# Rotary embedding in fp32: part of one store on GpSimd's queue, and three rows in one GpSimd product

## The chip, the cores and the metric

The kernel runs on one core of a Trainium2 chip. Such a core has four engines that compute (TensorE, VectorE, ScalarE, GpSimd), a SyncE that issues transfers here, and sixteen DMA engines that move the data. In the profile these are PE (and PEld for its weight loads), DVE, ACT, POOL and SP. The metric is the device time of one execution in microseconds (us), lower is better. The time before is the median of three runs.

## The reference

The input `x` is 16 batches of 512 positions of 1024 numbers in fp32, that is, 16 heads of 64. In each head the first 32 numbers and the last 32 are rotated against each other by tables that depend on the position alone:

```python
x = x.reshape(batch, seq, num_heads, head_dim)          # 16, 512, 16, 64
x1, x2 = (x[..., :half_dim], x[..., half_dim:])
cos = cos[None, :, None, :]                             # from (512, 32)
sin = sin[None, :, None, :]
rotated = np.concatenate([x1 * cos - x2 * sin, x1 * sin + x2 * cos], axis=-1)
```

32 MiB come in, 32 MiB go out, with two products and one sum for each number.

## The kernel before

The kernel cuts the work into 8 tiles of 4 MiB. A tile has 128 partitions (2 batches by 64 groups of positions), and a partition has 8 rows (positions) of 1024 numbers, 32 KB in all. Five tiles are held at a time. Loads and stores are issued by SyncE, in the order of the program:

```python
NB, BUFS, BANK = 2, 5, 512
PAIRS = ((1, 2), (4, 5), (6, 7))
EXTRA = 5

xp = ...tile_pool(name="xp", bufs=BUFS)                 # tiles of x, 32 KB a partition
bp = ...tile_pool(name="bp", bufs=3)                    # products with sin, 8 KB a partition

load(0, 0, FIRST[0])                                    # rows 0 to 2 of tile 0
... sin and cos tables, the other rows of tile 0 ...
for t in range(1, BUFS):
    load(t)                                             # tiles 1 to 4
spare = fixed.tile([1, EXTRA, 16], FP32)
for i in range(EXTRA):                                  # transfers of 64 bytes
    nc.sync.dma_start(out=spare[:1, i], in_=sin_v[:1, :16])
```

The identity matrix that TensorE needs is made by GpSimd. TensorE spreads the tables over 128 partitions and VectorE writes the signed sine table (L116, L117); GpSimd's products wait for that.

The work on one tile is split by rows. For the pairs of rows (1, 2), (4, 5) and (6, 7) GpSimd multiplies the swapped halves by the sine (`sin_rows`, L165), VectorE multiplies by the cosine into PSUM (`pair_product`, L141) and adds the two (`pair_sum`, L189). Row 3 gets its sine product from GpSimd too; VectorE's cosine product goes into a half-row PSUM buffer, TensorE adds GpSimd's product to it by a matmul with the identity, and ScalarE copies the sum back (`pe_half`, one half of the row at a time, one buffer). Row 0 does without GpSimd. The order in a tile:

```python
for t in range(NT):
    first, second, third = PAIRS
    b1 = sin_rows(t, first[0], 2)
    p1 = pair_product(t, first[0])
    ... row 0: VectorE's product, TensorE's sums, ScalarE's copy ...
    b3 = sin_rows(t, ROW_PE, 1)                         # row 3
    b2 = sin_rows(t, second[0], 2)                      # rows 4 and 5
    pair_sum(*p1, b1)
    h0, h1 = zip(parts(rows(t, ROW_PE)), parts(b3))
    pe_half(ROW_PE, *h0)
    p2 = pair_product(t, second[0])
    b1 = sin_rows(t, third[0], 2)                       # rows 6 and 7
    pair_sum(*p2, b2)
    pe_half(ROW_PE, *h1)
    p1 = pair_product(t, third[0])
    if t + 1 < NT:
        cos_product(own_ps, rows(t + 1, ROW_OWN), ROW_OWN)
    pair_sum(*p1, b1)
    stores(t)

def stores(t):                                          # cut: one store of the whole tile
    store(t, 0, KK)
    if t + 1 == NT - BUFS:                              # after store 2
        for n in range(BUFS, NT):
            load(n)                                     # tiles 5, 6 and 7
```

So the transfers follow each other as: loads 0 to 4, stores 0 to 2, loads 5 to 7, stores 3 to 7.

Of the kernel before, what the change touches and what calls it, by code (L numbers as in the profile page):

```python
# [8 lines left out]
FP32 = mybir.dt.float32  # L9
BF16 = mybir.dt.bfloat16  # L10
# [4 lines left out]
BANK = 512  # L15


ROW_OWN, ROW_PE = 0, 3

PAIRS = ((1, 2), (4, 5), (6, 7))  # L20

FIRST = (3, 8)
LAST_OUT = (8,)

EXTRA = 5


@with_exitstack
def kernel(
# [13 lines left out]
    nc = tc.nc  # L43
    P = nc.NUM_PARTITIONS
    batch, seq, dim = x.shape
# [3 lines left out]
    PB = P // NB  # L49
    KK = seq // PB  # L50
    NT = batch // NB
    F = KK * dim

    x_v = x.rearrange("(t b) (p k) d -> t (b p) (k d)", b=NB, k=KK)
    out_v = out.rearrange("(t b) (p k) h d -> t (b p) (k h d)", b=NB, k=KK)
    cos_v = cos.rearrange("(p k) j -> p (k j)", k=KK)
    sin_v = sin.rearrange("(p k) j -> p (k j)", k=KK)

    fixed = ctx.enter_context(tc.tile_pool(name="fixed", bufs=1))
    xp = ctx.enter_context(tc.tile_pool(name="xp", bufs=BUFS))  # L60
    bp = ctx.enter_context(tc.tile_pool(name="bp", bufs=3))
    pfix = ctx.enter_context(tc.tile_pool(name="pfix", bufs=1, space=bass.MemoryType.PSUM))
    pe = ctx.enter_context(tc.tile_pool(name="pe", bufs=1, space=bass.MemoryType.PSUM))
    pd = ctx.enter_context(tc.tile_pool(name="pd", bufs=1, space=bass.MemoryType.PSUM))
# [3 lines left out]
    tiles = [None] * NT  # L68

    def load(t, lo=0, hi=KK):  # L70
        if tiles[t] is None:
            tiles[t] = xp.tile([P, F], FP32, name="xt")
        s = slice(lo * dim, hi * dim)
        nc.sync.dma_start(out=tiles[t][:, s], in_=x_v[t][:, s])  # L74

    def store(t, lo=0, hi=KK):
        s = slice(lo * dim, hi * dim)
        nc.sync.dma_start(out=out_v[t][:, s], in_=tiles[t][:, s])

    load(0, 0, FIRST[0])  # L80
    tabs = bp.tile([P, 2 * dim], FP32, name="b")
# [3 lines left out]
    nc.sync.dma_start(out=cos_sb, in_=cos_v)  # L85
    for lo, hi in zip(FIRST, FIRST[1:]):
        load(0, lo, hi)
    for t in range(1, BUFS):
        load(t)
    spare = fixed.tile([1, EXTRA, 16], FP32)  # L90
    for i in range(EXTRA):
        nc.sync.dma_start(out=spare[:1, i], in_=sin_v[:1, :16])

    ident = fixed.tile([P, P], FP32)
    make_identity(nc, ident)
    zero = fixed.tile([P, BANK], BF16)
    nc.vector.memset(zero, 0.0)  # L97
    own_ps = pe.tile([P, dim], FP32)
    pe_ps = pe.tile([P, BANK], FP32)
    for ps in (own_ps[:, :BANK], own_ps[:, BANK:], pe_ps):  # L100
# [3 lines left out]
    tab = pfix.tile([P, BANK], FP32)  # L104
    cos_t = tab[:, : KK * half]
    sin_t = tab[:, KK * half : 2 * KK * half]
    spread = fixed.tile([PB, P], FP32)
    eye = ident[:PB, :PB]
    nc.vector.tensor_copy(
        out=spread.rearrange("p (b q) -> p b q", b=NB),  # L110
        in_=bass.AP(tensor=eye.tensor, offset=eye.offset, ap=[eye.ap[0], [0, NB], [1, PB]]),
# [12 lines left out]
    def swapped(r):  # L124
        n = r.shape[1] // hd
        return bass.AP(tensor=r.tensor, offset=r.offset + half, ap=[r.ap[0], [hd, n], [-half, 2], [1, half]])

    def rows(t, k, n=1):
        return tiles[t][:, k * dim : (k + n) * dim]

    def cos_product(out, r, k, n=1):

        c = cos_t[:, k * half : (k + n) * half]
        m = r.shape[1] // (n * half)
        if n == 1:
            cb = bass.AP(tensor=c.tensor, offset=c.offset, ap=[c.ap[0], [0, m], [1, half]])
            o, i = (z.rearrange("p (a j) -> p a j", j=half) for z in (out, r))
        else:
            cb = bass.AP(tensor=c.tensor, offset=c.offset, ap=[c.ap[0], [half, n], [0, m], [1, half]])
            o, i = (z.rearrange("p (k a j) -> p k a j", k=n, j=half) for z in (out, r))  # L140
        nc.vector.tensor_tensor(out=o, in0=i, in1=cb, op=ALU.mult)  # L141

    def own_product(r):

        s = bass.AP(
            tensor=own_t.tensor,
            offset=own_t.offset + half,
            ap=[own_t.ap[0], [0, nh], [-half, 2], [1, half]],
        )
        nc.vector.tensor_tensor(out=heads(r), in0=heads(r), in1=s, op=ALU.mult)  # L150

    def sin_product(out, r, k, n):
        s = sns[:, k : k + n].rearrange("p k a j -> p (k a j)")
        if n == 1:
            sb = bass.AP(tensor=s.tensor, offset=s.offset, ap=[s.ap[0], [0, nh], [1, hd]])
            o, i = heads(out), swapped(r)
        else:
            sb = bass.AP(tensor=s.tensor, offset=s.offset, ap=[s.ap[0], [hd, n], [0, nh], [1, hd]])
            o = out.rearrange("p (k h a j) -> p k h a j", k=n, a=2, j=half)
            i = bass.AP(  # L160
                tensor=r.tensor,
                offset=r.offset + half,
                ap=[r.ap[0], [dim, n], [hd, nh], [-half, 2], [1, half]],
            )
        nc.gpsimd.tensor_tensor(out=o, in0=i, in1=sb, op=ALU.mult)  # L165

    def sin_rows(t, k, n):
        b = bp.tile([P, 2 * dim], FP32, name="b")[:, : n * dim]
        sin_product(b, rows(t, k, n), k, n)
        return b  # L170

    def parts(r):
        return [r[:, i * BANK : (i + 1) * BANK] for i in range(r.shape[1] // BANK)]

    def pe_add(ps, other):
        nc.tensor.matmul(out=ps, lhsT=ident, rhs=other, start=False, stop=True, skip_group_check=True)  # L176

    def pe_half(k, r, b):
        cos_product(pe_ps, r, k)
        pe_add(pe_ps, b)  # L180
        nc.scalar.copy(out=r, in_=pe_ps)  # L181

    def pair_product(t, k):
        ps = pd.tile([P, 2 * dim], FP32, name="pd")
        cos_product(ps, rows(t, k, 2), k, 2)
        return ps, rows(t, k, 2)

    def pair_sum(ps, r, b):
        nc.vector.tensor_tensor(out=r, in0=ps, in1=b, op=ALU.add)  # L189

    def stores(t):
        lo = 0
        for hi in LAST_OUT if t == NT - 1 else (KK,):
            store(t, lo, hi)
            lo = hi
        if t + 1 == NT - BUFS:
            for n in range(BUFS, NT):
                load(n)

    cos_product(own_ps, rows(0, ROW_OWN), ROW_OWN)  # L200
    for t in range(NT):
        first, second, third = PAIRS
        b1 = sin_rows(t, first[0], 2)
        p1 = pair_product(t, first[0])
        r0 = rows(t, ROW_OWN)
        own_product(r0)
        for ps, r in zip(parts(own_ps), parts(r0)):
            pe_add(ps, swapped(r))
        nc.scalar.copy(out=r0, in_=own_ps)  # L209
        b3 = sin_rows(t, ROW_PE, 1)  # L210
        b2 = sin_rows(t, second[0], 2)
        pair_sum(*p1, b1)
        h0, h1 = zip(parts(rows(t, ROW_PE)), parts(b3))
        pe_half(ROW_PE, *h0)
        p2 = pair_product(t, second[0])
        b1 = sin_rows(t, third[0], 2)
        pair_sum(*p2, b2)
        pe_half(ROW_PE, *h1)
        p1 = pair_product(t, third[0])
        if t + 1 < NT:  # L220
# [3 lines that stand above are left out]
# [35 lines left out]
```

## Time and profile before

| | before |
|---|---|
| time, median of 3 (range) | 162.52 us (162.47 to 162.65) |
| span of the profiled execution | 160.7 us |
| DVE busy | 136.3 us, 85% |
| POOL busy | 127.2 us, 79% |
| PE busy | 56.4 us, 35% |
| ACT busy | 18.1 us, 11% |
| DMA, share of 16 engines | 97.9% |
| bytes moved | 67.25 MB in 2619 packets |

The times in the profile are counted from the start of the span. A group of instructions is named by its line in the kernel, its engine and its operation, with what it writes and reads; then come its busy time, the mean of one instruction, and the idle time of the engine just before it with the instruction that ended most of it. A DMA share of 1.00 means that all sixteen DMA engines have a packet under way. A packet here is the row of one partition, 32 KB in a transfer of a whole tile.

### The profile page before, as it was taken

To read this page: it belongs to the slowest core of one execution; us is meant where nothing else is said; L and a number is where in the kernel's file an instruction comes from. 1 tells how busy PE (TensorE), PEld (TensorE's weight loads), DVE (VectorE), ACT (ScalarE), POOL (GpSimd) and SP (SyncE) were. 2 spreads that over 40 slices of the span, in tenths; PEclk is the share of its full clock that TensorE was granted. 3 is DMA by queue.
4 is the path that set the end of the run, shared out by engine and by line. 5 is a ranking of instruction groups with operands and counts; after the bars stand their busy time and mean duration, and the time that the engine had idled before them with its cause. 6 is when DMAs were issued, how large, how long until landed. Compare 5 with 4: busy or idle time off the path is not lost.

```text
span 160.7 us, 443 instructions
## 1 busy us (share of the span) xinstructions
PE 56.4 (35%) x71; PEld 18.8 (12%) x71; DVE 136.3 (85%) x85; ACT 18.1 (11%) x25; POOL 127.2 (79%) x38
## 2 busy tenths in 40 slices
PE   3131905064503731191309150745046402822000
PEld 0111301021102210121004010211021101210000
DVE  1059969999999999999999999999999999998000
ACT  0001311003000301021100310031003010201000
POOL 1049999999999999988998899898999899840000
PEclk9999985559555865567555855595558655675555
DMA  5999999999999999999999999999999999999993
GB/s 180 407 408 473 392 498 416 392 457 457 392 416 481 408 400 498 408 392 506 410 392 473 432 400 449 457 400 416 489 392 408 498 400 408 481 416 400 392 514 139
DMA packets 2619, 67.25 MB, mean 419 GB/s; under 512 B 314, under 2 KB 442, under 8 KB 442
## 3 DMA queue, kind: packets, MB, share of 16 engines
q1 hardware_dynamic: 2618, 67.24, 97.9%
q14 instruction: 1, 0.01, 0.0%
HBM read 33.69 MB, written 33.55 MB: 418 GB/s over the span
## 4 chain that ended last, share of the span: by engine, by line
DVE 68%; issue 12%; POOL 6%; DMA 4%; PE 1%; SPq 0%; DVEq 0%
DVE xt L189 33%; DVE pd L141 31%; POOL b L165 6%; DMA b<-in_sin_dram 4%; DVE pe_ps L141 3%; PE tab L113 1%; PE tab L114 1%; DVE sns L116 0%; DVE xt L150 0%; DVE own_ps L141 0%; SPq L74 0%; DVE sns L117 0%; DVEq L189 0%
## 5 line engine op out<-in xcount | busy, mean ns | idle before, releaser
L165 POOL TENSOR_TENSOR b<-xt,sns 128x2048 f32<-128x2048 f32 (+1 forms) x32 | 126.5, 3987 | 14.5 <-DVE sns L117 9.1
L189 DVE TENSOR_TENSOR xt<-pd,b 128x2048 f32<-128x2048 f32 x24 | 54.9, 2287 | 2.4 <-POOL b L165 1.6
L141 DVE TENSOR_TENSOR pd<-xt,tab 128x2048 f32<-128x2048 f32 x24 | 55.0, 2291 | 0.2
L176 PE MATMUL own_ps<-xt,ident 128*128 128x512 f32 x32 | 29.1, 1064 | 54.0 <-DVE xt L150 48.3
L176 PE MATMUL pe_ps<-b,ident 128*128 128x512 f32 x32 | 25.2, 880 | 29.1 <-DVE pe_ps L141 29.1
L176 PEld LDWEIGHTS own_ps<-xt,ident 128*128 128x128 f32 x32 | 9.4, 324 | 74.0 <-DVE xt L150 59.3
L209 ACT COPY xt<-own_ps 128x1024 f32<-128x1024 f32 x8 | 8.1, 1013 | 72.2 <-PE own_ps L176 72.2
L181 ACT COPY xt<-pe_ps 128x512 f32<-128x512 f32 x16 | 9.4, 589 | 40.7 <-PE pe_ps L176 40.7
L176 PEld LDWEIGHTS pe_ps<-b,ident 128*128 128x128 f32 x32 | 8.0, 279 | 43.8 <-DVE pe_ps L141 36.0
L141 DVE TENSOR_TENSOR pe_ps<-xt,tab 128x512 f32<-128x512 f32 x16 | 11.0, 686 | 0.0
L141 DVE TENSOR_TENSOR own_ps<-xt,tab 128x1024 f32<-128x1024 f32 x8 | 9.8, 1223 | 0.0
L150 DVE TENSOR_TENSOR xt<-xt,tab 128x1024 f32<-128x1024 f32 x8 | 9.7, 1214 | 0.0
L116 DVE TENSOR_SCALAR sns<-tab 128x256 f32<-128x256 f32 x1 | 0.4, 426 | 8.0 <-PE tab L114 8.0
L209 ACT ACT_TABLE_LOAD x1 | 1.3, 1283 | 15.3 <-DVE xt L150 15.3
L113 PE MATMUL tab<-b,spread 64*128 64x256 f32 x2 | 1.2, 697 | 4.9 <-DMA b<-in_sin_dram 4.9
L101 PE MATMUL own_ps<-zero 128*128 128x512 bf16 x2 | 1.0, 622 | 1.2 <-DVE zero L97 1.2
L113 PEld LDWEIGHTS tab<-b,spread 64*128 64x128 f32 x2 | 0.5, 308 | 5.7 <-issue 5.7
L114 PE MATMUL tab<-b,spread 64*128 64x256 f32 x2 | 1.1, 631 | 0.0
L97 DVE MEMSET zero<- 128x256 uint32 x1 | 0.3, 272 | 0.9 <-PEq L240 0.9
L114 PEld LDWEIGHTS tab<-b,spread 64*128 64x128 f32 x2 | 0.7, 333 | 0.2
L101 PE MATMUL pe_ps<-zero 128*128 128x512 bf16 x1 | 0.6, 634 | 0.0
L101 PEld LDWEIGHTS <-zero 128*128 128x128 bf16 x3 | 0.3, 125 | 1.5 <-DVE zero L97 1.2
(9 smaller groups left out, 1.8 us busy)
## 6 DMA issues: line engine op xcount, KB each, us to landing
out_dram<-xt SPq DMA_DIRECT2D x8, 4096.0 KB, 21.4
xt<-in_x_dram SPq DMA_DIRECT2D x7, 4096.0 KB, 38.8
xt<-in_x_dram SPq DMA_DIRECT2D x1, 2560.0 KB
xt<-in_x_dram SPq DMA_DIRECT2D x1, 1536.0 KB
spare<-in_sin_dram SPq DMA_DIRECT2D x5, 0.1 KB
b<-in_sin_dram SPq DMA_DIRECT2D x1, 64.0 KB
b<-in_cos_dram SPq DMA_DIRECT2D x1, 64.0 KB
```

Source lines behind the costliest of these rows:

```text
L97: nc.vector.memset(zero, 0.0)
L101: nc.tensor.matmul(out=ps, lhsT=zero[:, :P], rhs=zero, start=True, stop=True)
L113: nc.tensor.matmul(out=sin_t, lhsT=spread, rhs=sin_sb, start=True, stop=True)
L114: nc.tensor.matmul(out=cos_t, lhsT=spread, rhs=cos_sb, start=True, stop=True)
L116: nc.vector.tensor_scalar_mul(out=sns[:, :, 0, :], in0=sin_k, scalar1=-1.0)
L141: nc.vector.tensor_tensor(out=o, in0=i, in1=cb, op=ALU.mult)
L150: nc.vector.tensor_tensor(out=heads(r), in0=heads(r), in1=s, op=ALU.mult)
L165: nc.gpsimd.tensor_tensor(out=o, in0=i, in1=sb, op=ALU.mult)
L176: nc.tensor.matmul(out=ps, lhsT=ident, rhs=other, start=False, stop=True, skip_group_check=True)
L181: nc.scalar.copy(out=r, in_=pe_ps)
L189: nc.vector.tensor_tensor(out=r, in0=ps, in1=b, op=ALU.add)
L209: nc.scalar.copy(out=r0, in_=own_ps)
```

## The change

Two things are changed. First, the store of tile 3 is cut into pieces. The rows of the first 112 partitions are stored as before, and so are the first 12 KB of the last 16 partitions. Of the other 20 KB of these 16 partitions, those of 13 partitions are issued by GpSimd on its software queue (in front of its products for tile 5), those of two partitions by SyncE, and those of the last one by SyncE in two transfers of 16 runs of 640 bytes. A small transfer of 3 partitions is issued by GpSimd at the very start. The purpose is to choose which DMA engines carry these pieces. The spare transfers of SyncE go from five to one, so that the number of transfers ahead of the later ones stays in step.

Second, GpSimd multiplies rows 3, 4 and 5 in one instruction in place of two. Its result has a buffer of its own of three rows, whose room comes from one of the three buffers of two rows and from two small tiles that now lie in it at the start. The purpose is fewer GpSimd instructions.

```diff
+GROUPS = ((1, 2), (3, 3), (6, 2))
-EXTRA = 5
+EXTRA = 1
+SHARED, LAST_P, AHEAD, CUT = 3, 16, 13, 3072
...
-    bp = ctx.enter_context(tc.tile_pool(name="bp", bufs=3))
+    bp = ctx.enter_context(tc.tile_pool(name="bp", bufs=2))
+    bp3 = ctx.enter_context(tc.tile_pool(name="bp3", bufs=1))
...
+    three = fixed.tile([P, 16], FP32)
+    nc.gpsimd.dma_start(out=three[: LAST_P - AHEAD], in_=sin_v[: LAST_P - AHEAD, :16])
     ident = fixed.tile([P, P], FP32)
     make_identity(nc, ident)
-    zero = fixed.tile([P, BANK], BF16)
+    for _ in range(5):
+        nc.gpsimd.nop(hint="pause")
+    early = bp3.tile([P, 3 * dim], FP32, name="b3")
+    zero = early[:, : BANK // 2].bitcast(BF16)
...
-    spread = fixed.tile([PB, P], FP32)
+    spread = early[:PB, BANK : BANK + P]
...
     def sin_rows(t, k, n):
-        b = bp.tile([P, 2 * dim], FP32, name="b")[:, : n * dim]
+        b = bp.tile([P, 2 * dim], FP32, name="b") if n == 2 else bp3.tile([P, 3 * dim], FP32, name="b3")
...
+    def store_shared(t):
+        a, b, c = P - LAST_P, P - LAST_P + AHEAD, P - 1
+        for q, s in (
+            (slice(a), slice(F)),
+            (slice(a, P), slice(CUT)),
+            (slice(b, c), slice(CUT, F)),
+        ):
+            nc.sync.dma_start(out=out_v[t][q, s], in_=tiles[t][q, s])
+        o, i = (z[c:P, CUT:].rearrange("p (e a n) -> p e a n", e=16, a=2) for z in (out_v[t], tiles[t]))
+        for n in range(2):
+            nc.sync.dma_start(out=o[:, :, n], in_=i[:, :, n])
+
+    def store_ahead(t):
+        q, s = slice(P - LAST_P, P - LAST_P + AHEAD), slice(CUT, F)
+        nc.gpsimd.dma_start(out=out_v[t][q, s], in_=tiles[t][q, s])
...
     def stores(t):
+        if t == SHARED:
+            store_shared(t)
+            return
...
+        if t == SHARED + 2:
+            store_ahead(SHARED)
-        b1 = sin_rows(t, first[0], 2)
+        b1 = sin_rows(t, *GROUPS[0])
...
-        b3 = sin_rows(t, ROW_PE, 1)
-        b2 = sin_rows(t, second[0], 2)
+        b2 = sin_rows(t, *GROUPS[1])
         pair_sum(*p1, b1)
-        h0, h1 = zip(parts(rows(t, ROW_PE)), parts(b3))
+        h0, h1 = zip(parts(rows(t, ROW_PE)), parts(b2[:, :dim]))
         pe_half(ROW_PE, *h0)
         p2 = pair_product(t, second[0])
-        b1 = sin_rows(t, third[0], 2)
-        pair_sum(*p2, b2)
+        b1 = sin_rows(t, *GROUPS[2])
+        pair_sum(*p2, b2[:, dim:])
```

## The prediction

> **What bounds the kernel now.** I read the page from the top, then the chain of waits, then the stretches of time, then single transfers. The first look goes to the DMA rows and the queue row.
>
> ```profile
> span 160.7 us, 443 instructions
> ...
> DMA  5999999999999999999999999999999999999993
> ...
> q1 hardware_dynamic: 2618, 67.24, 97.9%
> ...
> HBM read 33.69 MB, written 33.55 MB: 418 GB/s over the span
> ```
>
> The sixteen DMA engines are busy from the second slice to the last but one. The bytes are fixed: the whole input in, the whole output out. So the kernel is a stream with a head and a tail, and the chain of waits, which names VectorE for 68% of the span, must be read beside that. The chain in order of time shows how VectorE runs:
>
> ```profile
> 10.44 3.33 POOL b L165
> 13.77 1.14 issue
> 14.91 6.85 POOL b L165 x2
> 21.78 2.29 DVE xt L189
> ...
> 145.80 2.29 DVE xt L189
> ```
>
> At 21.78 us VectorE starts the sum of rows 4 and 5 of tile 0, after its only real wait on GpSimd (1.57 us), and from there it has no gap until 145.80 + 2.29 = 148.09 us. The stretches around that moment (length, then busy time and count for PE, PEld, DVE, ACT and POOL, then granted clock, DMA share, GB/s) are:
>
> ```profile
> 21.78:148.09 126.31, 47.92 (x58) 15.57 (x58) 125.24 (x74) 15.20 (x22) 115.13 (x29) 0.60 1.00 431
> 148.09:149.00 0.91, 0.00 (x0) 0.00 (x0) 0.00 (x0) 0.00 (x0) 0.00 (x0) 0.50 0.43 180
> 149.00:159.30 10.30, 0.00 (x0) 0.00 (x0) 0.00 (x0) 0.00 (x0) 0.00 (x0) 0.50 0.92 394
> 159.30:160.70 1.40, 0.00 (x0) 0.00 (x0) 0.00 (x0) 0.00 (x0) 0.00 (x0) 0.50 0.00 0
> ```
>
> DVE is busy 125.24 of 126.31 us and the DMA share is 1.00: two bounds run side by side and meet at 148 us. (Packets are counted where they start, hence 0.43.) The last store is issued at 148.15 us. For the packets I used the trace's own records: each packet's start, time and size, and each engine's completion of a transfer. Packets laid end to end make sixteen chains, one per engine. Ten of the chains stand idle for 0.08 to 0.54 us before the last store's first packets at 148.98 to 149.16 us, so on most engines VectorE's end sets the end. One chain is different: it is still 0.97 us behind the median after the store before, and ends its last packet at 159.51 us, where the other fifteen end between 158.74 and 159.00. It lost the time in three packets of a row of 32 KB, 1.507 us (at 50.7), 1.651 us (at 80.1) and 1.462 us (at 109.6), where the ordinary one takes 1.213 us, and in many of a few ns. The last store's sixteen completions say the same: fourteen at 159.07 to 159.27 us, one at 159.45, one at 159.84, and the span ends 0.83 us after that last one. **So the end is set by one late DMA engine; 0.39 us behind it stands a second; 0.57 us behind it the fourteen that VectorE fed.**
>
> [...]
>
> **Part 1, the store of tile 3.** Before, every engine carries 8 rows of 32 KB. After, as I read the diff: 112 partitions, 7 whole rows for each engine; the first 12 KB of the last 16 partitions, one for each engine; and of their other 20 KB, 13 go through the software queue, 2 through the hardware queue[...], and one is cut into 32 runs of 640 B, two for each engine. [...] Engine 2 alone gets none. By bytes: engine 2 carries 7 x 32 + 12 + 1.25 = 237.25 KB instead of 256, the other fifteen 257.25. At 1.213 us for 32 KB, 18.75 KB less are 0.71 us; 1.25 KB more are 0.05 us. The pieces also bring more completion writes (four or five in place of one, 9 ns each and about 6 ns between packets), some 0.06 us for everyone. Net: engine 2 gains about 0.65 us, the others lose about 0.1. That 0.65 so nearly equals the 0.57 us by which the late chain trails the fourteen that I take engine 2 to be the late one; the trace can't confirm it. The fourteen mostly have an idle stretch before the last store to lose 0.1 us in.
>
> With that, the late engine completes at 159.84 - 0.65 = 159.19 us, and the end passes to the second, 159.45 us plus up to 0.1. Gain: 159.84 - 159.50 = **0.34 us**.
>
> **Part 2, one GpSimd product for rows 3 to 5.** From the groups kept apart by shape:
>
> ```profile
> L165 POOL TENSOR_TENSOR b<-xt,sns 128x2048 f32<-128x2048 f32 x24 | 108.4, 4530 | 14.5 <-DVE sns L117 9.1 <-DVE xt L189 5.4
> L165 POOL TENSOR_TENSOR b<-xt,sns 128x1024 f32<-128x1024 f32 x8 | 18.9, 2360 | 0.0
> ```
>
> A row costs 4530 - 2360 = 2170 ns, the fixed part is 190 ns, so three rows in one are 6700 ns against 2360 + 4530 = 6890. Eight times 190 ns are 1.5 us of GpSimd, all beside VectorE, except in tile 0, where VectorE waits for this very product: 21.78 becomes about 21.6. Against it, row 3 is ready only then instead of at 17.3 us. TensorE must add it (1.44 us for the pair of matmuls here in tile 0) and ScalarE copy it (0.59 us) before VectorE may overwrite that PSUM buffer: 21.6 + 1.44 + 0.59 + some 0.2 of hand-offs = 23.85, and VectorE comes to it at about 21.6 + 2.2 = 23.8. A tie: from -0.15 to +0.3 us, I take **+0.05**. In later tiles VectorE needs 16.97 us and GpSimd 2 x 4.53 + 6.70 = 15.8, so GpSimd gains over 1 us per tile. The single three-row buffer comes free when TensorE has added the second half of row 3, some 12.6 us after VectorE began the tile (five steps of 2.2, 1.2, 2.2, 0.6 and 2.2 us lead up to the sum of rows 4 and 5 at 8.4, then 2.2 for it, 0.6 for the half, 1.4 for TensorE). The next one is wanted at 17.0 + 8.4 = 25.4, so 12.8 us stay for a product of 6.7. It doesn't bind.
>
> **Part 3, the rest.** GpSimd's store of 13 rows is issued in front of tile 5's products, by when GpSimd is several us ahead; [...]all hidden. The 20 KB packets (0.76 us each for that size in the first load) delay the loads of tiles 5 to 7 on thirteen engines, but the last of these lands at 110.8 us and VectorE takes tile 7 up at 132. Four spare transfers fewer let store 0 be issued at about 30.3 instead of 33.2 us; it only joins a queue that is full until load 4 lands at 52.6. The early 3-partition transfer precedes the identity matrix, which isn't wanted before 7.5 us. Sum: -0.34 + 0.05, or 162.52 - 0.3 = **162.2 us**.
>
> **Rivals.** (a) *The late engine isn't engine 2, or another one is late in another execution.* Then nothing is relieved, the late engine carries 0.1 us more: 162.6. [...] (b) *The software queue places its 13 rows on engines 0 to 12.* Then 0 and 1 carry 20 KB more, 0.76 + 0.1 us, of which their idle stretch takes 0.1 to 0.5: 162.4 to 162.8. (c) *A software transfer costs more than the trace of before can tell*, at the start (VectorE's tables 0.5 us later moves the end almost by as much) or in small packets: 162.8 to 163.5. (d) *VectorE becomes the bound*, if the tie of part 2 goes wrong: another +0.3, 162.5. (e) All goes well and the second late engine's 0.2 us was chance: 161.9.
>
> **Range and chances.** I give the mechanism about 60%: 161.9 to 162.3. The rivals spread from 162.4 to 163. So 161.7 to 162.9. Two per cent are 3.25 us. No part can save that, since the relief is bounded by the 0.57 us between the late engine and the others; a loss of that size needs a stall that nothing here shows.
>
> **What would show it.** Right: the sixteen completions of the last store within 0.4 us; VectorE's end within 0.3 us of 148.09; GpSimd's three-row products near 6700 ns; one chain of packets short of a 20 KB packet, and that the one with long packets. Wrong: the late chain still there (rival a), two chains with two 20 KB packets (b), a late first product or a gap before the end in DVE (c, d).

## The result and the profile after

The changed kernel takes 167.29 us, the one before 162.5: a ratio of 1.029 (95% interval 1.026 to 1.031). One of its four runs, at 173.5 us and with a lower granted clock (0.625), was in a slower state and is left out of the ratio. The prediction was 162.2, from 161.7 to 162.9. The change costs 4.8 us where it was to save 0.3.

First the rows of the page, with GB/s in forty slices of 4.14 us:

```profile
span 165.5 us, 444 instructions
...
DMA  5999989898999898999989899999999999999960
GB/s 193 417 436 475 412 388 499 380 507 380 451 436 380 380 507 380 459 428 404 477 388 483 381 459 412 467 412 420 324 347 444 412 451 420 436 443 420 459 261 24
...
q1 hardware_dynamic: 2694, 66.98, 95.9%
q0 software_dynamic: 64, 0.27, 0.4%
```

The bytes are the same, and the new queue carries its 0.27 MB. Two places stand out in GB/s: 324 and 347 in the slices from 115.9 to 124.1 us, and 261 and 24 at the end. The DMA row says 9 in the former: the engines were busy and moved less. The chain of waits, in order of time, tells whether VectorE has anything to do with it:

```profile
14.84 6.69 POOL b L176
21.55 2.29 DVE xt L200
...
145.57 2.29 DVE xt L200
```

It hasn't. VectorE starts at 21.55 instead of 21.78 us and ends at 147.86 instead of 148.09. The three-row products, in the groups kept apart by shape, are as worked out:

```profile
L176 POOL TENSOR_TENSOR b<-xt,sns 128x2048 f32<-128x2048 f32 x16 | 72.1, 4523 | 10.6 <-DVE sns L128 7.8 <-DMA xt<-in_x_dram 2.8
...
L176 POOL TENSOR_TENSOR b<-xt,sns 128x3072 f32<-128x3072 f32 x8 | 53.5, 6684 | 1.0 <-PE pe_ps L187 1.0
```

So the loss is in the transfers alone. The stretches around the store of tile 3 place it (the last two numbers of a line are the DMA share and GB/s). First the kernel before:

```profile
110.00:114.00 4.00, 1.68 (x2) 0.10 (x1) 4.00 (x3) 0.59 (x1) 4.00 (x2) 0.50 1.16 500
114.00:118.00 4.00, 0.00 (x0) 0.00 (x0) 3.97 (x3) 0.00 (x0) 4.00 (x2) 0.50 0.93 401
118.00:122.00 4.00, 3.42 (x4) 1.46 (x5) 4.00 (x4) 0.00 (x0) 3.53 (x2) 0.50 0.95 410
122.00:126.00 4.00, 1.14 (x3) 0.19 (x1) 3.90 (x3) 1.50 (x2) 3.32 (x2) 0.93 1.08 467
```

and the changed one:

```profile
110.00:114.00 4.00, 1.45 (x2) 0.00 (x0) 4.00 (x3) 0.58 (x1) 4.00 (x2) 0.50 0.97 401
114.00:118.00 4.00, 0.00 (x0) 0.00 (x0) 3.96 (x3) 0.00 (x0) 4.00 (x1) 0.50 1.04 393
118.00:122.00 4.00, 3.65 (x5) 1.62 (x6) 4.00 (x4) 0.00 (x0) 4.00 (x2) 0.53 0.98 312
122.00:126.00 4.00, 0.86 (x3) 0.03 (x1) 3.90 (x3) 1.50 (x2) 4.00 (x2) 0.90 0.96 384
```

Over these sixteen microseconds the changed kernel moves 373 GB/s on average where the other moves 445, and it is lowest, 312, from 118 us on. The trace's packet records show it transfer by transfer. From about 111 us, when the 112-partition piece of the store of tile 3 begins, packets of 32 KB last up to 2.918 us instead of 1.213: 27 of those that start between 108 and 130 us last over 1.3 us (2 in the kernel before), and all that start in that time are together 19.9 us too long (0.7 before). Packets of 12 KB, of the piece with 16 partitions, last up to 1.958 us instead of 0.460.

The engines come out of this store unevenly, and stay so. The sixteen completions of the four stores after it lie 5.34, 5.34, 5.36 and 5.35 us apart from first to last, which fits engines that each have the same work in every later store. Of the last store the first completes at 159.25 us (before: 159.07), the median at 160.72 (159.14), the last at 164.60 (159.84). **The median engine lost 1.6 us; the kernel waits for the slowest, which lost 4.8.** The two last ones, at 163.77 and 164.60 us, are by their order the two engines that carried SyncE's piece of two rows of 20 KB. These two packets took 2.261 and 2.712 us, where the ordinary one of this size takes 0.761. After the piece of 16 partitions the last engine was 2.13 us behind the median, after this one 4.25. The third from last completes the last store at 162.40 us, so some 2.2 of the 4.8 us came with that piece. The stretches of the tail show the waiting:

```profile
147.86:159.30 11.44, 0.00 (x0) 0.00 (x0) 0.00 (x1) 0.00 (x0) 0.00 (x0) 0.50 0.98 424
159.30:165.50 6.20, 0.00 (x0) 0.00 (x0) 0.00 (x0) 0.00 (x0) 0.00 (x0) 0.50 0.17 74
```

After 159.30 us, where no packet starts any more in the kernel before, 74 GB/s go on for a few engines, with a DMA share of 0.17.

### The profile page after: what moved, and what is told of

Its sections match the earlier page's. It is cut to its first block, busy times and chain, and to the rows that moved or that the text cites. A ratio compares the mean times of both kernels' runs of the same rounds, so it can differ in the third digit from the quotient of the medians.

```text
span 165.5 us, 444 instructions
## 1 busy us (share of the span) xinstructions
PE 56.2 (34%) x71; PEld 18.3 (11%) x71; DVE 136.3 (82%) x85; ACT 18.2 (11%) x25; POOL 126.9 (77%) x32
## 4 chain that ended last, share of the span: by engine, by line
DVE 58%; POOL 14%; issue 9%; PE 4%; DMA 4%; SPq 0%; DVEq 0%; POOLq 0%
DVE xt L200 29%; DVE pd L152 25%; POOL b L176 14%; DVE pe_ps L152 4%; DMA b<-in_sin_dram 4%; PE pe_ps L187 3%; PE tab L124 1%; PE tab L125 1%; DVE sns L127 0%; SPq L80 0%; DVE sns L128 0%; DVE own_ps L152 0%; DVE xt L161 0%; DVEq L200 0%; POOLq L176 0%
## 5 line engine op out<-in xcount | busy, mean ns | idle before, releaser
L176 POOL TENSOR_TENSOR b<-xt,sns 128x2048 f32<-128x2048 f32 (+1 forms) x24 | 125.0, 5243 | 11.6 <-DVE sns L128 7.8
L187 PEld LDWEIGHTS pe_ps<-b,ident 128*128 128x128 f32 x32 | 7.5, 268 | 44.2 <-DVE pe_ps L152 32.9
L124 PE MATMUL tab<-b,b 64*128 64x256 f32 x2 | 1.2, 697 | 4.8 <-DMA b<-in_sin_dram 4.8
L112 PE MATMUL own_ps<-b 128*128 128x512 bf16 x2 | 1.0, 621 | 1.2 <-DVE b L108 1.2
L101 POOL DMA_DIRECT2D three<-in_sin_dram x1 | 0.7, 704 | 0.8 <-POOLq L271 0.8
L124 PEld LDWEIGHTS tab<-b,b 64*128 64x128 f32 x2 | 0.5, 307 | 5.7 <-issue 5.7
L125 PE MATMUL tab<-b,b 64*128 64x256 f32 x2 | 1.1, 632 | 0.0
L125 PEld LDWEIGHTS tab<-b,b 64*128 64x128 f32 x2 | 0.7, 334 | 0.2
```

The costliest lines, as they stand in the source:

```text
L101: nc.gpsimd.dma_start(out=three[: LAST_P - AHEAD], in_=sin_v[: LAST_P - AHEAD, :16])
L112: nc.tensor.matmul(out=ps, lhsT=zero[:, :P], rhs=zero, start=True, stop=True)
L124: nc.tensor.matmul(out=sin_t, lhsT=spread, rhs=sin_sb, start=True, stop=True)
L125: nc.tensor.matmul(out=cos_t, lhsT=spread, rhs=cos_sb, start=True, stop=True)
```

## The experiments

Theory A was formed from this trace, in which the rows of the piece of 112 partitions take up to 2.918 us and the 12 KB of the piece of 16 up to 1.958, where a store of 128 partitions has 1.213 for a row and a packet of 12 KB ordinarily takes 0.460. So theory A is that the pieces of the store of tile 3 that name fewer than 128 partitions cause the loss; why they should, the trace doesn't show. Theory B blames the software queue or the small runs, theory C the GpSimd product and its single buffer, theory D any further transfer. Theory R is the premise of the prediction: that the change relieves the late engine. All edits are to the kernel before unless something else is said; one spare transfer was taken out for each transfer added to the store.

**One part alone.** The edit is the second part of the change, as in the diff above, with the store left whole.

```diff
-        b3 = sin_rows(t, ROW_PE, 1)
-        b2 = sin_rows(t, second[0], 2)
+        b2 = sin_rows(t, *GROUPS[1])
```

> The kernel before with the second part of the change alone: rows 3 to 5 in one GpSimd product, with its buffer; the store of tile 3 is whole and no software transfer is there. Theory A (the pieces of the store of tile 3 cause the loss[...]): 162.2 to 162.6. Theory C (the GpSimd product or its single buffer causes it): 166 to 168.

Measured: 162.37 us, ratio 0.9997 (0.9987 to 1.0006). Theory C falls; the part is neutral, as predicted.

**The cut alone, on the hardware queue.**

```diff
-            store(t, 0, KK)
+            for q, s in ((slice(112), slice(F)), (slice(112, P), slice(F))):    # tile 3
+                nc.sync.dma_start(out=out_v[t][q, s], in_=tiles[t][q, s])
```

> The kernel before with one edit: the store of tile 3 is cut into 112 partitions and 16 partitions, both whole rows on SyncE's hardware queue (one spare transfer fewer, to keep the number of transfers). No software queue, no small runs, no new GpSimd product. Theory A: slower, 166 to 170, with long packets from the moment this store starts. Theory B (the software transfer, or the runs of 640 bytes, cause the loss): 162.4 to 162.8. Theory D (every further transfer costs something fixed): 162.5 to 163.5.

Measured: 169.34 us, ratio 1.044 (1.042 to 1.046). The stretches where it is lost:

```profile
114.00:118.00 4.00, 0.00 (x0) 0.00 (x0) 3.97 (x3) 0.00 (x0) 4.00 (x2) 0.50 1.01 377
118.00:122.00 4.00, 3.41 (x4) 1.46 (x5) 4.00 (x4) 0.00 (x0) 3.53 (x2) 0.50 1.29 254
122.00:126.00 4.00, 1.63 (x3) 0.34 (x1) 3.90 (x3) 1.60 (x2) 3.33 (x1) 0.87 0.66 262
```

254 and 262 GB/s, with packets up to 7.9 us. There is no software queue and no small run here, so neither is needed for the loss, and a cut into two plain pieces is enough. It costs more than the change does; here the 16 partitions go out with whole rows among the other stores.

**As many pieces, cut by columns.**

```diff
+            for q, s in ((slice(P), slice(3072)), (slice(P), slice(3072, F))):  # tile 3
```

> The kernel before with one edit: the store of tile 3 is cut by columns, 128 partitions of 12 KB and then 128 partitions of 20 KB. As many transfers as in the cut by 112 and 16 partitions[...]. Theory A: no loss, 162.4 to 162.8. Theory D (a cut as such costs): as slow as the cut by partitions.

Measured: 162.44 us, ratio 1.0004 (0.9993 to 1.0014). Theory D falls. The same stretches hold their rate:

```profile
114.00:118.00 4.00, 0.00 (x0) 0.00 (x0) 3.96 (x3) 0.00 (x0) 4.00 (x2) 0.50 0.99 424
118.00:122.00 4.00, 3.47 (x4) 1.47 (x5) 4.00 (x4) 0.00 (x0) 3.52 (x2) 0.50 0.99 428
122.00:126.00 4.00, 1.53 (x3) 0.34 (x1) 3.90 (x3) 1.60 (x2) 3.33 (x2) 0.89 1.12 483
```

**Two halves of the partitions.** That each half takes up to twice its time was the author's estimate; no trace before this run showed it.

```diff
+            for q, s in ((slice(64), slice(F)), (slice(64, P), slice(F))):      # tile 3
```

> The kernel before with one edit: the store of tile 3 is cut into partitions 0 to 63 and 64 to 127. [...] Theory A: the two halves take up to twice their time, 9.7 us more in all, so 170 to 173, with packets of 32 KB near 2.4 us. If only an uneven share of partitions costs (7 to an engine)[...]: 162.5 to 163, since 64 divides by 16.

Measured: 170.42 us, ratio 1.049 (1.047 to 1.051).

```profile
114.00:118.00 4.00, 0.00 (x0) 0.00 (x0) 3.96 (x3) 0.00 (x0) 4.00 (x2) 0.50 0.97 221
118.00:122.00 4.00, 3.23 (x4) 1.46 (x5) 4.00 (x4) 0.00 (x0) 3.52 (x2) 0.50 1.03 221
122.00:126.00 4.00, 1.76 (x3) 0.34 (x1) 3.90 (x2) 1.60 (x2) 3.52 (x1) 0.86 1.07 213
```

Half the rate, for as long as the store lasts, and the most common long packet takes 2.548 us, 2.10 times 1.213. Every piece of this cut and of the one by 112 and 16 has sixteen completions, and 64 is a multiple of 16 like 128, so as far as the completions show it needs no uneven share to cost. The 12 KB packets of the changed kernel take up to 4.3 times their ordinary time (1.958 us against 0.460), the 32 KB packets of the cut by 112 and 16 up to 6.5 times theirs (7.9 against 1.213). A cut by partitions also changes which rows of the output in DRAM are written at one time, and no run separates that from the partitions that are read. What is shown is that the cut by partitions costs; the reason isn't.

**A smaller dose.** The cut by 112 and 16 for the last 4 KB of each partition only.

```diff
+            for q, s in ((slice(P), slice(7168)), (slice(112), slice(7168, F)), (slice(112, P), slice(7168, F))):
```

> The cut by 112 and 16 partitions applied to the last row of tile 3 alone (4 KB of 32); its first seven rows go out as 128 partitions. Theory A: the loss goes with the bytes[...], so about an eighth of the 6.9 us that the cut of whole rows cost: 163.0 to 163.8. If a transfer under 128 partitions costs a fixed amount: 167 to 170 again.

Measured: 163.26 us, ratio 1.0064 (1.0049 to 1.0079), so 1.0 us against 6.9 for whole rows. A fixed cost of every transfer under 128 partitions falls. An eighth of 6.9 us would be 0.9, but the trace doesn't show the loss spread over the bytes: 122 of the 128 packets of 4 KB took 0.159 us, about an eighth of 1.213, and only two took three times that, 0.479 and 0.476. The last store's median completion, 159.17 us, is as before. What changed is the last engine: it is 0.57 us behind the median when the 128-partition piece is done and 1.50 us when the piece of 112 is done. So one engine bore nearly the whole loss, and the agreement with an eighth shows no proportion.

**The software queue alone.** The store of tile 3 stays whole; the 13 rows go out once more, into a place that the last store writes again.

```diff
+        # cut: the early 3-partition transfer and the pauses, as in the change
+        if t == 5:
+            nc.gpsimd.dma_start(out=out_v[7][112:125, 3072:], in_=tiles[3][112:125, 3072:])
```

> The kernel before with the software queue's part alone: the 3-partition transfer and the five pauses at the start, and GpSimd's store of the same 13 partitions by 20 KB of tile 3, in front of its products for tile 5, but into the place of tile 7's output, which the last store writes again later. The store of tile 3 stays whole. 13 engines carry 20 KB more. Theory A[...]: 162.4 to 163.4, the 0.76 us of the bytes at most. Theory B (the software queue delays the stream or GpSimd): over 165.

Measured: 163.61 us, ratio 1.0081 (1.0065 to 1.0098): 1.4 us, more than the 0.76 us of the bytes and a little above theory A's range. In the trace the last completion is at 160.58 us, 0.74 later than before, and the span ends 1.26 us after it instead of 0.83. So it seems that the late engine itself got one of the rows (a probe below shows it), and 0.43 us came after the last completion, for a reason that is open. (The changed kernel has only 0.90 us there.) Theory B falls as the cause of the 4.8 us.

**The changed kernel without the software queue.** All pieces are issued by SyncE; the early transfer and the pauses are gone, and here no spare transfer was taken out.

```diff
-        nc.gpsimd.dma_start(out=out_v[t][q, s], in_=tiles[t][q, s])
+        nc.sync.dma_start(out=out_v[t][q, s], in_=tiles[t][q, s])    # 13 x 20 KB, ahead of the other pieces
```

> The changed kernel with the 13 partitions by 20 KB issued by SyncE with the other pieces, and no software transfer at all. Theory A: still slow, 167 to 170; somewhat slower than the changed kernel[...]. Theory B: back at 162.4 to 163.5.

Measured: 173.53 us, ratio 1.068 (1.066 to 1.071). That is 6.2 us slower than the changed kernel, and beyond the range that theory A had given. In the trace twelve of the 13 packets of 20 KB took 1.795 to 4.062 us and one 0.761. The software queue didn't cause the loss; by moving 13 rows to a time when only loads were under way it kept the loss smaller.

**Which engine is late, and which are spared.** The first probe put small loads ahead of everything, from ScalarE's queue.

```diff
+    for k in (1, *range(1, 16)):
+        nc.scalar.dma_start(out=tags[:k, k], in_=sin_v[:k, :8])
```

> A probe for the DMA engines' numbers, not for time. The kernel before with 16 small loads ahead of everything, issued by ScalarE, with 1 to 15 partitions of 32 bytes (and one more of 1). If a transfer of k partitions below 16 runs on the k lowest engines[...], the number of 32-byte packets in a chain tells its engine: 16 in engine 0, none in engine 15. Everything shifts by 5 to 10 us. Theory R (relieving engine 2 was meant for the late one, as the prediction took it): the late chain, the one with packets over 1.4 us near the middle and the end of the span, has 13 of them. Otherwise another number, and the prediction's step on engine 2 falls whatever else is found.

Measured: 168.0 us, all shifted. Two queues are at work at that time, and the chains couldn't be told apart for certain: the chain with the long packet at 80.8 us had 12 small packets, which would be engine 3, but the chain of engine 0 had 13 where 16 were due. It settles nothing. The second probe has five small loads between two large ones of the same queue.

```diff
+                    for j, k in enumerate((1, 2, 3, 4, 8)):                    # ahead of load 7
+                        nc.sync.dma_start(out=tags[:k, j], in_=sin_v[:k, :8])
```

> A second probe for the engines' numbers: the kernel before with five loads of 32 bytes a partition, with 1, 2, 3, 4 and 8 partitions, between the loads of tiles 6 and 7 on SyncE's queue, near 101 us. With k engines each, engine 0 carries five such packets, engine 1 four, engine 2 three, engine 3 two, engines 4 to 7 one, the others none. Theory R (the change relieves the late engine): the late chain carries three. If it carries another number, the change relieved an engine that wasn't late. Time: within 0.5 us of before.

Measured: 162.78 us. The late chain passes this place half a microsecond after all others, so that its records stand alone (start us, end us, ns, bytes; 4 bytes are completion writes):

```
101.155  101.164      9      4
101.161  101.170      9     32
101.167  101.176      9      4
101.172  101.181      9     32
101.178  101.187      9      4
```

Two packets of 32 bytes: it takes part in two of the five loads. The trace prints no engine numbers; counted as in the expectation, with a load of k partitions on engines 0 to k - 1, these are the loads of 4 and 8 partitions, and it is engine 3. This count is an assumption, and the numbers below rest on it too. The change meant to spare engine 2. Theory R falls.

> The same five loads in the kernel that adds the software queue's 13 rows. As the change is drawn up, the 13 software packets of 20 KB lie on the chains with two or fewer of the 32-byte packets (engines 3 to 15), and the three chains with 3, 4 and 5 have none. If the software queue starts its second transfer elsewhere, it is three other chains.

The same five loads in the kernel with 13 extra software rows (164.27 us): the three chains with no row carry no 32-byte packet, so they lie among engines 8 to 15; the late chain, again with two, has a row. It is the second alternative, three other chains than the change was drawn up for. Then five loads of 4, 12, 13, 14 and 15 partitions:

> The kernel with the software queue's 13 extra rows again, with the five small loads on 4, 12, 13, 14 and 15 partitions: five packets of 32 bytes in engines 0 to 3, four in 4 to 11, three in 12, two in 13, one in 14, none in 15. If the software rows lie on engines 0 to 12 whatever went before, the three chains without one carry two, one and none. If they start elsewhere (at 5, say), the spared chains carry four.

Measured: 164.03 us. The three spared chains carry two, one and none: engines 13, 14 and 15. With a first software transfer of 6 partitions in place of 3:

> The same with a first software transfer of 6 partitions in place of 3. If the first transfer moves the start of the second, as the change counts on, the spared chains change against the run before. If it doesn't, they are the same three.

Measured: 164.36 us, and again two, one and none. So the 13 rows lie on engines 0 to 12, whether the small transfer ahead of them has 3 partitions or 6. That its size moves their start, on which the change rested, was an assumption, and the two runs speak against it. In the trace of the changed kernel the software transfers of 3 and of 13 partitions have sixteen completions each, where SyncE's piece of two partitions has two, at 124.82 and 125.76 us. Why the rows lie where they do isn't shown.

**A relief beside a store of 128 partitions.** Before those last two runs a strip of 2.5 KB was taken from the store of tile 3, 120 partitions of it for the software queue, behind 4 or 3 partitions, to spare engine 3 or engine 2 on the same assumption.

```diff
+    nc.gpsimd.dma_start(out=start[:4], in_=sin_v[:4, :16])                      # [:3] in the control
+            nc.gpsimd.dma_start(out=out_v[3][:120, 7552:], in_=tiles[3][:120, 7552:])   # at t == 5
+            for q, c in ((slice(P), slice(7552)), (slice(120, P), slice(7552, F))):
```

> [...]in the kernel before, the last 2.5 KB of every partition of tile 3 leave the hardware store, which keeps all 128 partitions; 120 partitions of that strip go through the software queue at tile 5, while only loads are in the hardware queue, behind a first transfer of 4 partitions, so that they [...]spare engine 3, the late one by the second probe; the last 8 partitions go through the hardware queue (20 KB in all). Engine 3 carries 17.5 KB less, 0.65 us. If the late engine alone sets the end: 161.8 to 162.2. If the software queue costs at the end of the execution what the run with its 13 extra rows hints at (0.4 us beside its bytes): 162.2 to 162.6.

> The control: the same strip behind a first transfer of 3 partitions, so that it [...]spares engine 2, as the change meant to. If engine 3 is the late one: no gain, and 0.4 to 0.8 us slower than the version that spares engine 3, 162.4 to 163.0. If engine 2 were the late one: the order is the reverse.

Measured: 162.87 us, ratio 1.0035 (1.0021 to 1.0048), and 162.96 us, ratio 1.0042 (1.0029 to 1.0055). The expected gain isn't there, both lie above the ranges given for the first, and the two are alike. In both traces one stream of software packets starts at 96.36 and 96.41 us, where the others start between 95.4 and 96.0, and stays behind them as the late chain does, so the late engine had rows of the strip in both. Both traces have fifteen such streams, each of four packets of 5 KB: one engine of the sixteen was spared, and not the late one. Here too the span ends later after the last completion than before, by 1.28 and 1.26 us instead of 0.83. No version tried here beats the kernel before.

## Why the prediction was wrong

**What bounds the kernel: right.** Taking either bound apart changed what it should: the three-row product alone moved VectorE's end from 148.09 to 147.91 us and the last store's median completion from 159.14 to 158.99, but the time not at all (0.9997), and 20 KB more on the late engine moved the last completion by 0.74 us. How late that engine is varies: with the same bytes its last completion stands at 159.84 in the kernel before and at 160.59 in the profile of the cut by columns.

**Part 1, "by bytes": this step failed.** It added up the kilobytes of each engine and took each packet "at 1.213 us for 32 KB". That duration came from transfers of 128 partitions, the only large ones in the kernel before, and it doesn't hold for 112 (up to 2.918 us) or 16 (12 KB in up to 1.958). The cut by columns has the same bytes in every engine as before and loses nothing; the cuts by partitions, as far as their sixteen completions a piece show, give each engine the same bytes too and lose 6.9 and 8.0 us. The 0.1 us lost by fifteen engines was really 1.6 us on the median engine and 4.8 on the slowest, and the last completions, which were to lie within 0.4 us, lie 5.35 apart.

**Part 1, "engine 2 is the late one": failed as well, in both halves.** That engine 2 alone gets none of the 13 rows was assumed; nothing in the trace of before showed where software rows go. The near equality of 0.65 and 0.57 us was chance. By the count of the probes the late engine is number 3 in the two runs that could tell it, and the software rows leave out 13 to 15. Rival (b) had the right engines, 0 to 12, and said that 0 and 1 would carry 20 KB too many. The two engines with the extra piece of 20 KB did end last. But (b) gave that piece its ordinary 0.76 us, where it took 2.26 and 2.71, and left out what all engines lost. How the rest divides between the 112 rows, the 16 and the software rows isn't told apart.

**Part 2: right in the product's size and in that nothing waits for it.** 6684 ns against 6700, and VectorE at 21.55 against 21.6. VectorE's end is earlier by 0.23 us, just outside "-0.15 to +0.3". The single buffer did hold GpSimd twice, for 1.0 us in all (the wait for PE in its line among the groups), but VectorE had no new wait from it.

**Part 3: right in that it is hidden.** GpSimd issued its store in 0.56 us, and the 2.84 us that it then waited were for the load of tile 5.

**The range** left the result out because "a loss of that size needs a stall that nothing here shows". The kernel before couldn't show it: it holds no large transfer of that shape.

## What to carry to other kernels

In these runs a large store's rate depended on which partitions it named, and not only on its bytes and the number of engines: when such a transfer has to be cut, cut it along the columns and leave it all 128 partitions (162.44 us here, against 169.34 and 170.42 for the two cuts by partitions). Where the engines stay as far apart as here (5.34 to 5.36 us over four stores), one uneven transfer in the middle is paid for at the end by the slowest engine, so look at the spread of the completions and not at the mean rate. And before a share of work is moved to relieve one engine, mark the engines in a trace and see which is late.

## What was not expected of the hardware

- Thirteen software packets of 20 KB, all from partitions 112 to 124, mostly took 0.761 us each, the ordinary time (the longest 0.974), when they ran at once beside loads. Sent by SyncE at the head of the store, the same rows took 2.736 us in the median. The partitions are the same in both, so they alone don't explain the difference; nor does a cut by partitions slow every packet: of the 4 KB packets of the smaller dose 122 of 128 took 0.159 us. The reason is open.
- A late engine is in every trace here where the chains can be followed, with a long packet near 80 us and mostly another near 110 (1.651 and 1.462 us before; 1.653 and 1.567 with the second probe). Nothing was tried for its cause.
